# A hybrid decoder step: ScalarE's DMAs moved to GpSimd, the heads' query and key loads reordered and merged, and another pair of engines splitting the attention outputs

## The chip, the core and the metric

The kernel runs on one core of a Trainium2 chip. The metric is the device time of one execution in microseconds (us), from the median of several runs. The engines are TensorE (PE in the profile; PEld are its weight loads), VectorE (DVE), ScalarE (ACT), GpSimd (POOL) and SyncE (SP). Sixteen DMA engines serve the DMAs that SP, ACT and POOL issue.

## What is computed

One step of a one-layer decoder for 1024 prompt tokens and 64 sample tokens (8 sequences of 8) over a cache of 2048 keys: a half feed-forward block, then a mix of windowed softmax attention (12 heads of 64) and gated linear attention (GLA, 4 heads), then another half feed-forward block. All data is float32; matmuls run on float32r, each operand split into a high part and a remainder.

```python
def _half_ffn(x, gain, w1, w3, w2):
    h = _rmsnorm(x, gain)
    return x + 0.5 * ((jax.nn.silu(h @ w1) * (h @ w3)) @ w2)

z = h @ w_in                          # q, k, v, and the GLA inputs
logits = einsum(q, k) * Dh ** -0.5 + bias        # three dilated windows
p = jnp.exp(logits - lse[..., None])
o = einsum(p, v)                      # the windows' outputs merged by lse
```

## The kernel before

A tile framework allocates the buffers, puts a wait before each use of a buffer, and orders the instructions of every engine by a simulated timeline in which earlier code has priority. Inside one engine instructions run in the order so fixed. `_interleave` (L59) runs several generators beside each other, so that the work of one fills the gaps of another.

The time has four stages. Until about 821 us: the first feed-forward block and the norm. From 821 to 1244 us, the mix stage: `inputs` projects the tokens to q, k, v and gates (matmuls `psg`, L306), and `beside` does the sample attention at the same time. Here `turn_values` transposes the values on PE (`psv`), ACT copies them to SBUF (`v`, L431) and issues their stores `out_vp` (L439), `vnew` (L434) and `out_wv_s` (L435); `finish_gate` stores the gate `zr` to `gsc` from ACT (L446); `finish_qk` stores q and k to `qsc` and `out_kT` from POOL (L473). `beside` loads its bias tile `sbias` (L799) from SP with a source of shape 8 x 16 x 1288 whose first dimension has stride zero, so that 16 rows are copied 8 times; and it issues `sko` and `soT` stores from ACT.

From 1244 to 1519 us, the attention stage, `attention` (12 prompt heads) runs beside `linear_states` (GLA). For each head `load(h)` brings q from `qsc` and k from `out_kT` (L929), each twice, as two DMAs of 64 rows by 1024 floats into the lower and the upper half of one 128-row tile `f`. There is one `f` buffer for q and one for k. DVE rounds them (`q`, L932; `kk`, L934) and POOL subtracts the remainders (L933, L935; DVE does that for the first head). Then come the bias tile (L937) and, for every even head, the values `va` of a pair (L940). `load(h + 1)` is called while head h works on the second of its four groups. `linear_states` loads its tiles `g` (L596, L598) on the same SP queue, and DVE's first use of them is L611. DVE does the bias and the running minimum of the scores (L969), ACT the exponentials. When a pair has four groups of output `o`, `split` writes the high part into `hH` (L132, DVE) and the remainder into `hL` (L134, DVE).

From 1519 us `out_proj` (matmuls `pso`) reads `hH`, `hL` and its weights `hl`, which ACT casts and POOL subtracts (L130, L134) from `raw`; the second feed-forward block follows until 2400 us.

Waits for DMAs are on semaphores. The DMAs of SP and ACT take turns on one set of eight, those of POOL on another set of eight; a DMA is issued only when the one before it on its semaphore has landed.

Of the kernel before, what the change touches and what calls it, by code (L numbers as in the profile page):

```python
# [9 lines left out]
F32 = mybir.dt.float32  # L10
# [6 lines left out]
P = 128  # L17
NT = 1088
NP = 1024
# [66 lines left out]
class _Weights:  # L86
# [6 lines left out]
    def load(self, j, k=0, nk=8):  # L93
        if j < len(self.units):
            if k == 0:
                self.raw[j] = self.pool.tile(list(self.units[j].shape), F32, tag="raw", name="raw", bufs=self.deep)
            self.k.nc.sync.dma_start(out=self.raw[j][:, k : k + nk], in_=self.units[j][:, k : k + nk])
# [23 lines left out]
class _Kernel:  # L121
# [299 lines left out]
    def turn_values(self, pool, ps, z, m, ci):  # L421
        nc, a = self.nc, self.a
        cols = slice(128 * m, 128 * m + 128)
        t0, nt = 3 * ci, 3 if ci < 2 else 2
        p = ps.tile([P, 512], F32, tag="b", name="psv")
        for t in range(nt):
            nc.tensor.transpose(p[:, 128 * t : 128 * t + 128], z[:, 128 * t : 128 * t + 128], self.ident)
        if ci == 2:
            nc.tensor.transpose(p[:64, 256:384], z[:, 256:320], self.ident)
        v = pool.tile([P, 3, 128], F32, tag="t1", name="v", bufs=4)  # L430
        nc.scalar.copy(v[:, :nt].rearrange("p t c -> p (t c)"), p[:, : 128 * nt])  # L431
        if ci == 2:
            nc.scalar.copy(v[:64, 2], p[:64, 256:384])
            nc.scalar.dma_start(out=self.vnew[:, cols], in_=v[:64, 2])  # L434
            nc.scalar.dma_start(  # L435
                out=a["wv_s"].rearrange("b (r c) -> b r c", c=768)[:, 2040:2048, cols], in_=v[:64, 2]
            )
            self.vdone = m + 1
        nc.scalar.dma_start(  # L439
            out=a["vp"][128 * t0 : 128 * (t0 + nt), cols].rearrange("(t p) c -> p t c", p=P), in_=v[:, :nt]  # L440
        )

    def finish_gate(self, z, m, ci):
        nc = self.nc
        nc.scalar.activation(z, z, AF.Silu)
        nc.scalar.dma_start(  # L446
            out=self.gsc[3 * ci : 3 * ci + 3, :, 5 + m].rearrange("t p r -> p t r"),
            in_=z.rearrange("p (t r) -> p t r", t=3),
        )
# [131 lines left out]
    def linear_states(self, pool, ps):  # L581

        nc, a = self.nc, self.a
        st = pool.tile([P, 9, 64], F32, tag="st", name="st", bufs=2)
        nc.gpsimd.memset(st[:, 0], 0.0)
        ms = pool.tile([P, 3, 36], F32, tag="gms", name="gms")
        qm = []
        for z in range(2):
            t = pool.tile([P, 4, 8, 32], F32, tag="qm", name="qm", bufs=2)
# [46 lines left out]
        for T in range(9):  # L636
            g, kdT, bl = nxt
# [9 lines left out]
            p = ps.tile([P, 512], F32, tag="T", name="psR", bufs=4)  # L647
            for j, src in enumerate((kdT, g[:, 3], g[:, 4])):
# [3 lines left out]
                out=kx,  # L652
# [9 lines left out]
            p = ps.tile([P, 512], F32, tag="T", name="psD", bufs=4)  # L662
# [115 lines left out]
    def sample(self, pool, ps, loadk):  # L778
# [18 lines left out]
        for i in range(6):  # L797
# [8 lines left out]
            for e in range(2):  # L806
# [7 lines left out]
            nc.tensor.transpose(p[:64, :128], ks, self.ident)  # L814
            ko = pool.tile([64, 128], F32, tag="sko", name="sko", bufs=1)
            nc.scalar.copy(ko, p[:64, :128])
            nc.scalar.dma_start(
                out=a["wk"].rearrange("b (r c) -> b r c", c=768)[:, 2040:2048, 128 * i : 128 * i + 128], in_=ko
            )
            e = pool.tile([P, NKEY], F32, tag="se", name="se", bufs=1)  # L820
# [83 lines left out]
            t = pool.tile([64, 8, 2, 8], F32, tag="soT", name="soT", bufs=1)  # L904
            nc.scalar.copy(t, p[:64, :128].rearrange("p (b e t) -> p b e t", e=2, t=8))
            for e in range(2):
                nc.scalar.dma_start(
                    out=self.osc[i, 64 * e : 64 * e + 64].rearrange("p (b t) -> p b t", t=8), in_=t[:, :, e]
                )
            yield 100  # L910

    def attention(self, inputs, pool, ps):
        nc = self.nc
        heads = {}

        def load(h):
            i, e = h // 2, h % 2
            f = []  # L920
            for u, src in enumerate((self.qsc, self.a["kT"])):
                f.append(inputs.tile([P, NP], F32, tag="f", name="f", bufs=2))
                if u == 0:
                    q = inputs.tile([P, NP], F32R, tag="q", name="q", bufs=2)
                    b = inputs.tile([P, NP], F32, tag="bias", name="bias", bufs=2)
                    kk = inputs.tile([P, 2, NP], F32R, tag="kk", name="kk", bufs=2)
                    kh, kl = kk[:, 0], kk[:, 1]
                for w in range(2):
                    nc.sync.dma_start(out=f[u][64 * w : 64 * w + 64], in_=src[64 * h : 64 * h + 64])  # L929
            o = slice(64, 128)  # L930
            el = nc.gpsimd if h else nc.vector
            nc.vector.tensor_copy(q, f[0])  # L932
            el.tensor_tensor(out=q[o], in0=f[0][o], in1=q[o].bitcast(F32), op=ALU.subtract)  # L933
            nc.vector.tensor_copy(kh, f[1])  # L934
            el.tensor_tensor(out=kl, in0=f[1], in1=kh.bitcast(F32), op=ALU.subtract)  # L935
            z = self.Z[h]
            nc.sync.dma_start(out=b, in_=bass.AP(z.tensor, z.offset + 127, [[GW - 1, P], [1, NP]]))  # L937
            if e == 0:
                v = pool.tile([P, 8, 128], F32, tag="v", name="va", bufs=2)
                nc.sync.dma_start(  # L940
                    out=v, in_=self.a["vp"][:, 128 * i : 128 * i + 128].rearrange("(t p) c -> p t c", p=P)
                )
            else:
                v = heads[h - 1][3]
            heads[h] = (q, kh, kl, v, b)

        def scores(h, g):

            q, kh, kl, v, b = heads[h]
            out = []  # L950
            ss = pool.tile([P, 2, 4], F32, tag="s", name="s", bufs=6)
            for n in (2 * g, 2 * g + 1):
                w = 128 * (n + 1)
                e = pool.tile([P, w], F32, tag=f"e{n}", name="e", bufs=2 if n < 4 else 1)
                s = ss[:, n % 2]
                out.append((e, s, w))
                for j, o in enumerate(range(0, w, 512)):
                    m = min(512, w - o)
                    mm = max(m, 256)
                    p = ps.tile([P, 512], F32, tag="S", name="psS", bufs=2)  # L960
                    for x, kk in enumerate((kh, kl)):
                        self.mm(  # L962
                            p[:, :mm],
                            lhsT=q[:, 128 * n : 128 * n + 128],
                            rhs=kk[:, o : o + mm],
                            start=x == 0,
                            stop=x == 1,
                        )
                    nc.vector.tensor_tensor_reduce(  # L969
                        out=e[:, o : o + m],  # L970
                        in0=p[:, :m],
                        in1=b[:, 128 * (7 - n) + o : 128 * (7 - n) + o + m],
                        op0=ALU.add,
                        op1=ALU.min,
                        scale=-1.0,
                        scalar=BIG if j == 0 else s[:, 0:1],
                        accum_out=s[:, j : j + 1],
                    )
                    yield None
            for e, s, w in out:  # L980
                j = (w - 1) // 512
                nc.scalar.activation(  # L982
                    e[:, :w], e[:, :w], AF.Exp, scale=-1.0, bias=s[:, j : j + 1], accum_out=s[:, 2:3]
                )
            yield [e for e, s, w in out] + [ss]
# [23 lines left out]
        def weigh(h, g, es, pts):  # L1009
            i, e = h // 2, h % 2  # L1010
            r = slice(64 * e, 64 * e + 64)
            v = heads[h][3]
            if g % 2 == 0 and e == 0:
                outs[i, g // 2] = pool.tile([P, 512], F32, tag="o", name="o", bufs=3)
            p = ps.tile([P, 512], F32, tag="O", name="psO", bufs=2)
# [16 lines left out]
                nc.vector.tensor_tensor(out=outs[i, g // 2][r, c], in0=p[o, :128], in1=rb[o], op=ALU.mult)  # L1032
            if g % 2 and e == 1:
                z = slice(512 * (g // 2), 512 * (g // 2) + 512)
                self.split(outs.pop((i, g // 2)), self.hH[:, i, z], self.hL[:, i, z], eh="dve", el="dve")

        order = [(h, g) for h in range(12) for g in range(4)]
        lag = 3
        outs = {}
        self.tc.keep_in_program_order(nc.scalar.preload_act_table_set(LOG_EXP))  # L1040
        load(0)
        yield 10
        es = {}
        for x in range(len(order) + lag):
# [102 lines left out]
    def run(self):  # L1147
        nc, tc, a = self.nc, self.tc, self.a
        self.gready, self.done, self.vdone = False, 0, 0
        with ExitStack() as top:  # L1150
            self.dram = top.enter_context(tc.tile_pool(name="dram", bufs=1, space=DRAM))
            cp = top.enter_context(tc.tile_pool(name="const", bufs=1))
# [120 lines left out]
            with ExitStack() as hs:  # L1273
                hpool(hs)
                with ExitStack() as bs:
                    ip, gp = (bs.enter_context(pool(n)) for n in ("attin", "gst"))
                    ap = bs.enter_context(pool("att", side="right"))
                    ps0 = bs.enter_context(pool("ps", space=PSUM))
                    states = (4.6 * c for c in self.linear_states(gp, ps0))
                    _interleave(tc, [(self.attention(ip, ap, ps0), 0), (states, 0)])  # L1280
                with pool("wts") as wp, pool("xp", side="right") as xp:
                    w = _Weights(self, wp, [a["wout"][u] for u in range(4)] + w13b)
                    w.start()
# [163 lines left out]
```

## Time and profile before

| | before |
|---|---|
| median of 3 runs | 2398.7 us (2397.25 to 2399.25) |
| profiled execution | 2401.93 us |
| its span, first to last instruction | 2400.1 us |
| PE busy | 2341.4 us (98%) |
| DVE busy | 1155.9 us (48%) |
| ACT busy | 656.9 us (27%) |
| POOL busy | 408.3 us (17%) |
| mean granted PE clock | 0.989 |

A row of the timeline gives an instruction's start and length, its engine, line, operation, output and input, and in brackets the engine's idle time before it and what ended it. "ACTq" and "SPq" are the queues on which an engine issues DMAs. "PEclk" is the granted clock as a share of full speed. A share of the DMA engines can pass 1, since overlapping packets are each counted.

### The profile page before, as it was taken

How to read it: one execution, taken by the hardware profiler on the slowest of the kernel's cores; microseconds unless marked ns; L12 is line 12 of the kernel's file. 1: busy time of each engine (PE TensorE's matmuls, PEld its weight loads, DVE VectorE, ACT ScalarE, POOL GpSimd, SP SyncE). 2: the span in 40 equal slices, each digit the busy share in tenths (PEclk: the TensorE clock that was granted, in tenths of full speed). 3: DMA queues.
4: the chain of work that ended last, by engine and by line, in shares of the span. 5: the costliest groups of instructions: out<-in, count | busy, mean ns of one | idle time of the engine just before them, and what ended most of it. 6: DMA issues, size and time to landing. Idle time of an engine off the chain costs nothing.

```text
span 2400.1 us, 38321 instructions
## 1 busy us (share of the span) xinstructions
PE 2341.4 (98%) x16073; PEld 2215.0 (92%) x16073; DVE 1155.9 (48%) x2377; ACT 656.9 (27%) x1347; POOL 408.3 (17%) x303
## 2 busy tenths in 40 slices
PE   7999999999999998999989999999999999999999
PEld 6999999999999987978767767999999999999999
DVE  8452434344342753555538887435444342434333
ACT  5111020101101522545436666334111101020110
POOL 5011020101100400011103231333101101020100
PEclk9999999999999999999999999999999999999999
DMA  7346542524250334599865442414244243111002
GB/s 258 110 162 192 191 152 97 210 97 153 86 196 23 134 131 108 179 342 341 310 184 130 111 115 74 156 36 158 88 163 153 92 154 143 45 53 45 28 17 85
DMA packets 135261, 330.25 MB, mean 138 GB/s; under 512 B 25920, under 2 KB 105264, under 8 KB 127408
## 3 DMA queue, kind: packets, MB, share of 16 engines
q1 hardware_dynamic: 116464, 316.39, 38.7%
q10 hardware_dynamic: 16512, 5.11, 0.9%
q0 software_dynamic: 2112, 6.29, 0.7%
q8 instruction: 126, 2.06, 0.3%
q14 instruction: 47, 0.39, 0.0%
HBM read 300.55 MB, written 134.56 MB: 181 GB/s over the span
## 4 chain that ended last, share of the span: by engine, by line
PE 89%; DVE 5%; DMA 3%; ACT 2%; issue 1%; SPq 1%; POOL 0%; ACTq 0%; DVEq 0%; POOLq 0%
PE ps L306 42%; PE ps L257 21%; PE psg L306 12%; PE pso L306 4%; PE psO L1022 2%; PE psS L962 2%; PE psW L880 1%; PE psT L1001 1%; DMA vt<-in_vin 1%; PE psA L831 1%; DVE hL L155 1%; DVE e L969 1%; PE pss L459 1%; DMA f<-out_kT 0%; DVE rstd L170 0%
## 5 line engine op out<-in xcount | busy, mean ns | idle before, releaser
L306 PE MATMUL ps<-hH,hl 128*128 128x362 f32 (+1 forms) x4224 | 1044.1, 328 | 8.1 <-ACT hl L130 6.8
L306 PEld LDWEIGHTS ps<-hH,hl 128*128 128x128 f32 x4224 | 746.6, 188 | 12.4 <-ACT hl L130 6.7
L306 PE MATMUL ps<-hL,hl 128*128 128x362 f32 (+1 forms) x2112 | 691.5, 328 | 2.9 <-DVE hL L155 2.9
L257 PE MATMUL ps<-g,hl 128*128 128x362 f32 (+1 forms) x3168 | 529.2, 328 | 0.0
L257 PEld LDWEIGHTS ps<-g,hl 128*128 128x128 f32 x3168 | 527.0, 188 | 0.0
L134 POOL TENSOR_TENSOR hl<-raw,hl 128x1024 fp32r<-128x1024 f32 (+1 forms) x98 | 242.8, 2498 | 1223.3 <-ACT hl L130 1223.3
L306 PEld LDWEIGHTS ps<-hL,hl 128*128 128x128 f32 x2112 | 397.5, 188 | 4.9 <-DVE hL L155 3.9
L306 PE MATMUL psg<-hH,hl 128*128 128x384 f32 (+3 forms) x1200 | 312.4, 334 | 0.0
L262 DVE SCALAR_TENSOR_TENSOR xT<-ps,xT 128x362 f32<-128x362 f32 (+1 forms) x384 | 204.6, 534 | 200.3 <-PE ps L257 191.4
L217 ACT ACTIVATE t<-t 128x364 f32<-128x364 f32 x132 | 66.9, 508 | 786.0 <-DVE t L216 785.8
L218 DVE TENSOR_TENSOR t<-ps,rstd 128x364 f32<-128x364 f32 x132 | 70.6, 535 | 417.9 <-PE ps L306 417.9
L306 PEld LDWEIGHTS psg<-hH,hl 128*128 128x128 f32 (+1 forms) x1200 | 211.3, 186 | 12.8 <-issue 8.9
L306 PE MATMUL psg<-hL,hl 128*128 128x384 f32 (+3 forms) x600 | 200.1, 334 | 0.1
L130 ACT CAST hl<-raw 128x1024 fp32r<-128x1024 f32 (+2 forms) x148 | 124.1, 886 | 187.3 <-PE ps L306 109.9
L130 ACT CAST g<-t 128x364 fp32r<-128x364 f32 x132 | 65.2, 494 | 346.8 <-DVE t L219 346.8
L134 DVE TENSOR_TENSOR g<-t,g 128x364 fp32r<-128x364 f32 x132 | 107.1, 813 | 92.8 <-ACT g L130 92.5
L216 DVE TENSOR_TENSOR t<-ps,rstd 128x364 f32<-128x364 f32 x132 | 70.5, 535 | 156.6 <-PE ps L306 155.3
L306 PEld LDWEIGHTS psg<-hL,hl 128*128 128x128 f32 (+1 forms) x600 | 111.7, 186 | 9.3 <-issue 6.7
L134 DVE TENSOR_TENSOR hl<-raw,hl 128x384 fp32r<-128x384 f32 (+3 forms) x178 | 102.9, 587 | 23.9 <-ACT hl L130 19.9
L962 PE MATMUL psS<-kk,q 128*128 128x512 f32 (+2 forms) x288 | 92.2, 411 | 19.6 <-DVE s L969 11.9
L306 PE MATMUL pso<-hH,hl 128*128 128x362 f32 (+1 forms) x384 | 93.6, 325 | 0.2 <-DVE o L1032 0.2
L982 ACT ACTIVATE e<-e,s 128x128 f32<-128x128 f32 (+3 forms) x96 | 74.9, 780 | 43.7 <-DVE s L969 43.1
(205 smaller groups left out, 2007.2 us busy)
## 6 DMA issues: line engine op xcount, KB each, us to landing
out_wk<-in_ck SPq DMA_DIRECT2D x16, 3060.0 KB
out_wv_s<-in_cv SPq DMA_DIRECT2D x16, 3060.0 KB
kt<-in_kin SPq DMA_DIRECT2D x24, 1280.0 KB
vt<-in_vin SPq DMA_DIRECT2D x60, 512.0 KB
raw<-in_w13b SPq DMA_DIRECT2D x22, 1024.0 KB
raw<-in_w13a SPq DMA_DIRECT2D x21, 1024.0 KB
raw<-in_w2a SPq DMA_DIRECT2D x48, 192.0 KB
raw<-in_w2b SPq DMA_DIRECT2D x48, 192.0 KB
```

Source lines behind the costliest of these rows:

```text
L130: nc.scalar.copy(hi, x)
L134: e.tensor_tensor(out=lo, in0=x, in1=hi.bitcast(F32), op=ALU.subtract)
L155: nc.vector.scalar_tensor_tensor(out=self.hL[:, k, s], in0=x, scalar=g, in1=self.hH[:, k, s].bitcast(F32), op0=ALU.mult, op1=ALU.subtract)
L216: nc.vector.tensor_tensor(out=t1[:, :n], in0=p1[:, :n], in1=r, op=ALU.mult)
L217: nc.scalar.activation(t1[:, :n], t1[:, :n], AF.Silu)
L218: nc.vector.tensor_tensor(out=t3[:, :n], in0=p3[:, :n], in1=r, op=ALU.mult)
L257: self.mm(p[:, :n], lhsT=hl[:, wt, j, :], rhs=g[:, gp, :n], start=i == 0, stop=i == 3 * nf - 1)
L262: nc.vector.scalar_tensor_tensor(out=xs, in0=p[:, :n], scalar=0.5, in1=xs, op0=ALU.mult, op1=ALU.add)
L306: self.mm(p[:m, :n], lhsT=hl[:, wt, k, cs], rhs=h[:, k, h0 : h0 + n], start=i == 0, stop=i == 23)
L962: self.mm(p[:, :mm], lhsT=q[:, 128 * n : 128 * n + 128], rhs=kk[:, o : o + mm], start=x == 0, stop=x == 1,)
L982: nc.scalar.activation(e[:, :w], e[:, :w], AF.Exp, scale=-1.0, bias=s[:, j : j + 1], accum_out=s[:, 2:3])
L1022: self.mm(p[64 * n : 64 * n + 64, :128], lhsT=v[:, k, r], rhs=pts[k // 2][k, n], start=k == 0, stop=k == 2 * g + n, tile_position=(0, 64 * n),
```

## The change

- The stores that ACT issued in `turn_values`, `finish_gate`, and for `sko` and `soT` are issued by GpSimd: 18 `out_vp`, 6 `vnew`, 6 `out_wv_s`, 6 `zr`, 6 `sko` and 12 `soT`, 54 in all.
- The values' load stands in a function of its own. That of pair 0 is called at the start of `linear_states`, the others after the bias of their even head.
- Each head's q and k come in one DMA of 512 KB each instead of two of 256 KB. Its source has a first dimension of 2 with stride zero, so that the 64 rows are read twice.
- `load(0)` is given priority, and the GLA states come first in `_interleave`.
- The split of the attention outputs takes the defaults of `split`: the cast on ACT, the subtraction on GpSimd.

```diff
-            nc.scalar.dma_start(out=self.vnew[:, cols], in_=v[:64, 2])
-            nc.scalar.dma_start(
+            nc.gpsimd.dma_start(out=self.vnew[:, cols], in_=v[:64, 2])
+            nc.gpsimd.dma_start(
...
-        nc.scalar.dma_start(
+        nc.gpsimd.dma_start(
             out=a["vp"][128 * t0 : 128 * (t0 + nt), cols].rearrange("(t p) c -> p t c", p=P), in_=v[:, :nt]
...
         nc.scalar.activation(z, z, AF.Silu)
-        nc.scalar.dma_start(
+        nc.gpsimd.dma_start(
             out=self.gsc[3 * ci : 3 * ci + 3, :, 5 + m].rearrange("t p r -> p t r"),
...
         nc.gpsimd.memset(st[:, 0], 0.0)
+        self.load_v(pool, 0)
...
-                for w in range(2):
-                    nc.sync.dma_start(out=f[u][64 * w : 64 * w + 64], in_=src[64 * h : 64 * h + 64])
+                nc.sync.dma_start(
+                    out=f[u], in_=src[64 * h : 64 * h + 64].unsqueeze(0).broadcast_to([2, 64, NP])
+                )
...
-            if e == 0:
-                v = pool.tile([P, 8, 128], F32, tag="v", name="va", bufs=2)
-                nc.sync.dma_start(
...
+            if h % 2 == 0 and h:
+                load_v(i)
...
-                self.split(outs.pop((i, g // 2)), self.hH[:, i, z], self.hL[:, i, z], eh="dve", el="dve")
+                self.split(outs.pop((i, g // 2)), self.hH[:, i, z], self.hL[:, i, z])
...
-        load(0)
+        with self.tc.high_priority(offset=300):
+            load(0)
...
-                    _interleave(tc, [(self.attention(ip, ap, ps0), 0), (states, 0)])
+                    _interleave(tc, [(states, 0), (self.attention(ip, ap, gp, ps0), 0)])
```

How the order of the instructions changes is shown at three places. On SP at the start of the attention stage, before (`vt` are the cached values of the sample attention; L929 are the loads of `f`):

```order
L794 DMA vt<-in_vin 128x1024 x4
L940 DMA va<-out_vp 128x8x128 x2
L929 DMA f<-qsc 64x1024 x2
L929 DMA f<-out_kT 64x1024 x2
L937 DMA bias<-Z 128x1024
L596 DMA g_11144<-gsc 128x640
L598 DMA g_11144<-asc 128x4x128
```

and now:

```order
L795 DMA vt<-in_vin 128x1024 x4
L936 DMA f<-qsc 128x1x1024
L936 DMA f<-out_kT 128x1x1024
L946 DMA bias<-Z 128x1024
L917 DMA va<-out_vp 128x8x128
L597 DMA g_11129<-gsc 128x640
L599 DMA g_11129<-asc 128x4x128
```

The first head's loads stand ahead of the values, and two instructions take the place of four.

On ACT in the mix stage, at the second head pair's values, before:

```order
L431 COPY v<-psv 128x384
L543 ACTIVATE gd<-gd 128x648
L439 DMA out_vp<-v 128x3x128
L561 COPY band<-psL 128x18x11
L431 COPY v<-psv 128x256
L543 ACTIVATE gd<-gd 128x576
L433 COPY v<-psv 64x128
L439 DMA out_vp<-v 128x2x128
L434 DMA vnew<-v 64x128
L435 DMA out_wv_s<-v 8x8x128
```

and now:

```order
L431 COPY v<-psv 128x384
L543 ACTIVATE gd<-gd 128x648
L561 COPY band<-psL 128x18x11
L431 COPY v<-psv 128x256
L543 ACTIVATE gd<-gd 128x576
L433 COPY v<-psv 64x128
L543 ACTIVATE gd<-gd 128x504
L561 COPY band<-psL 128x18x10
```

No DMA stands between ACT's copies any more.

On ACT at the end of the attention stage (`hl<-raw` are the first weights of `out_proj`), before:

```order
L991 COPY dg<-s 128x128
L1004 COPY pt<-psT 128x512 x3
L1018 COPY rb<-psO 128x128
L130 CAST hl<-raw 128x1024 x4
L159 ACTIVATE rstd<-xT 128x364
```

and now:

```order
L998 COPY dg<-s 128x128
L1011 COPY pt<-psT 128x512 x3
L1025 COPY rb<-psO 128x128
L130 CAST hH<-o 128x512
L130 CAST hl<-raw 128x1024 x4
L159 ACTIVATE rstd<-xT 128x364
```

The last cast of an attention output stands ahead of the weights' casts. On POOL the last subtraction of an output stands ahead of the weights' subtractions in the same way.

## Rows read from the trace of the kernel before

**Rows 1.** Two stages: length, busy of PE, PEld, DVE, ACT, POOL; PEclk, DMA share, GB/s.

```profile
821.00:1244.00 423.00, 410.21 (x3041) 347.47 (x3039) 210.42 (x406) 168.63 (x352) 38.77 (x94) 0.98 0.69 232
1244.00:1519.00 275.00, 248.13 (x2903) 193.44 (x2903) 216.50 (x653) 181.36 (x479) 72.42 (x52) 0.94 0.41 112
```

**Rows 2.** Timeline of SP at the start of the attention stage.

```profile
1224.89 1.75 SPq L794 DMA_DIRECT2D vt<-in_vin  x4
1237.09 1.01 SPq L940 DMA_DIRECT2D va<-out_vp  x2
1238.26 6.00 SPq L929 DMA_DIRECT2D f<-qsc  x2
1245.28 1.11 SPq L929 DMA_DIRECT2D f<-out_kT  x2
```

**Rows 3.** Timeline of PE there, its first matmul of the stage.

```profile
1250.82 0.77 PE L962 MATMUL psS<-kk,q 128*128 128x256 f32 x2 [6.91 <-DVE kk L934]
```

**Rows 4.** DMA issues: count and KB of each.

```profile
f<-qsc SPq DMA_DIRECT2D x24, 256.0 KB
...
bias<-Z SPq DMA_DIRECT2D x12, 512.0 KB
...
va<-out_vp SPq DMA_DIRECT2D x6, 512.0 KB
...
g<-gsc SPq DMA_DIRECT2D x9, 320.0 KB
...
g<-asc SPq DMA_DIRECT2D x9, 256.0 KB
```

**Rows 5.** Timeline of SP, then three windows, around one sbias load (columns as rows 1).

```profile
929.23 11.89 SPq L575 DMA_DIRECT2D asc<-band  x4
941.22 3.91 SPq L799 DMA_DIRECT2D sbias<-sB  x1
...
942.00:945.00 3.00, 3.00 (x23) 3.00 (x23) 0.19 (x1) 0.00 (x0) 0.00 (x0) 1.00 0.52 18
946.60:948.80 2.20, 2.20 (x15) 2.20 (x14) 0.00 (x0) 0.00 (x0) 0.00 (x0) 1.00 0.54 131
954.00:957.00 3.00, 0.00 (x0) 0.00 (x0) 0.00 (x0) 0.00 (x0) 0.00 (x0) 0.50 1.03 412
```

**Rows 6.** Timelines of DVE and of SP inside the heads.

```profile
1327.12 0.29 DVE L611 TENSOR_TENSOR gw<-g 128x128 f32<-128x128 f32 x1 [2.10 <-DMA g<-gsc]
...
1336.73 0.69 DVE L932 CAST q<-f 128x1024 fp32r<-128x1024 f32 x1
...
1472.58 0.69 DVE L932 CAST q<-f 128x1024 fp32r<-128x1024 f32 x1
...
1340.27 1.10 SPq L929 DMA_DIRECT2D f<-qsc  x2
```

**Rows 7.** Timelines of ACT and PE in the mix stage, and POOL's line of stores there.

```profile
954.63 0.38 ACTq L439 DMA_DIRECT2D out_vp<-v  x1
...
957.51 0.48 ACT L431 COPY v<-psv 128x384 f32<-128x384 f32 x1 [20.20 <-DMA vt<-in_vin]
...
958.04 0.69 PE L427 MATMUL psv<-ident,zv 128*128 128x128 f32 x2 [8.77 <-ACT v L431]
...
L473 POOL DMA_DIRECT2D qsc<-z x18 | 10.0, 554 | 143.0 <-DVE z L468 143.0
```

**Rows 8.** DVE's two lines of the output split, 1244 to 1521 us: busy, mean ns.

```profile
L134 DVE TENSOR_TENSOR hL<-o,hH 128x512 fp32r<-128x512 f32 x12 | 15.1, 1259 | 0.1
...
L132 DVE CAST hH<-o 128x512 fp32r<-128x512 f32 x12 | 10.0, 832 | 0.1
```

**Rows 9.** Timelines of ACT, POOL and DVE at the end of the attention stage.

```profile
1516.21 3.92 ACT L130 CAST hl<-raw 128x1024 fp32r<-128x1024 f32 x4
...
1517.36 10.09 POOL L134 TENSOR_TENSOR hl<-raw,hl 128x1024 fp32r<-128x1024 f32 x4 [8.69 <-ACT hl L130]
...
1518.47 0.59 DVE L1032 TENSOR_TENSOR o<-psO,rb 64x128 f32<-64x128 f32 x2 [2.48 <-PE psO L1022]
```

More of the change, by code (lines that the diff above doesn't have):

```diff
@@ L816, in sample @@
             nc.scalar.copy(ko, p[:64, :128])
-            nc.scalar.dma_start(
+            nc.gpsimd.dma_start(
                 out=a["wk"].rearrange("b (r c) -> b r c", c=768)[:, 2040:2048, 128 * i : 128 * i + 128], in_=ko
@@ L906, in sample @@
             for e in range(2):
-                nc.scalar.dma_start(
+                nc.gpsimd.dma_start(
                     out=self.osc[i, 64 * e : 64 * e + 64].rearrange("p (b t) -> p b t", t=8), in_=t[:, :, e]
@@ L910, in sample, with load_v, attention @@
             yield 100
-    def attention(self, inputs, pool, ps):
+    def load_v(self, pool, i):
+        v = pool.tile([P, 8, 128], F32, tag="v", name="va", bufs=2)
+        self.nc.sync.dma_start(
+            out=v, in_=self.a["vp"][:, 128 * i : 128 * i + 128].rearrange("(t p) c -> p t c", p=P)
+        )
+        self.values[i] = v
+    def attention(self, inputs, pool, vpool, ps):
         nc = self.nc
@@ L927, in load @@
                     kh, kl = kk[:, 0], kk[:, 1]
-                for w in range(2):
-                    nc.sync.dma_start(out=f[u][64 * w : 64 * w + 64], in_=src[64 * h : 64 * h + 64])
+                nc.sync.dma_start(
+                    out=f[u], in_=src[64 * h : 64 * h + 64].unsqueeze(0).broadcast_to([2, 64, NP])
+                )
             o = slice(64, 128)
@@ L937, in load, with load_v @@
             nc.sync.dma_start(out=b, in_=bass.AP(z.tensor, z.offset + 127, [[GW - 1, P], [1, NP]]))
-            if e == 0:
-                v = pool.tile([P, 8, 128], F32, tag="v", name="va", bufs=2)
-                nc.sync.dma_start(
[L941 to L945, printed above, removed]
+            if h % 2 == 0 and h:
+                load_v(i)
+            heads[h] = (q, kh, kl, b)
+        def load_v(i):
+            self.load_v(vpool, i)
         def scores(h, g):
-            q, kh, kl, v, b = heads[h]
+            q, kh, kl, b = heads[h]
             out = []
@@ L1011, in weigh @@
             r = slice(64 * e, 64 * e + 64)
-            v = heads[h][3]
+            v = self.values[i]
             if g % 2 == 0 and e == 0:
@@ L1149, in run @@
         self.gready, self.done, self.vdone = False, 0, 0
+        self.values = {}
         with ExitStack() as top:
```

## The prediction

> **What bounds the kernel now.** The first view to read is the table of stages [rows 1]. TensorE is busy 410 of 423 us in the mix stage and 248 of 275 us in the attention stage; in the other two stages, which the change leaves alone, it hardly stops. So there are only two places where a change can win: 13 us of idle time in the mix stage and 27 us in the attention stage. Nobody else is near his limit there: VectorE has 216 of 275 us, and the DMA engines work at 0.41 of their capacity. The second thing to read is the largest single stop in either stage. In the mix stage it is 8.77 us, for ACT's copy of the values [rows 7]; at the start of the attention stage it is 6.91 us, for the first head's keys [rows 3]. The third is the DMA view, for what each load of the attention stage carries [rows 4], and the windows round a load of the sample bias [rows 5], which is the one load of the old kernel written like the new head loads.
>
> **The stores moved from ACT to GpSimd: -9 us.** ACT copied its values late, at 957.51, after 20.20 us without work; the row puts that down to a DMA of cached values, yet in ACT's own queue a store `out_vp` stands issued at 954.63, and the copy follows it [rows 7]. The store's turn came only when an earlier DMA of the shared set, a load of SP's, had landed. GpSimd's DMAs have a set of their own and ACT has no DMA left there, so the 8.77 us for which TensorE waited go. What is late next? The operands of those transposes were ready, so nothing I can see; I take 9 us, as the clock stands at 0.50 in that stop [rows 5] and recovers after it. The ends are 0, should the store's place be taken by a wait for a buffer, and 11. The other side: 54 stores go to GpSimd. Its own stores cost 554 ns each [rows 7]; at that price they add 30 us, and at four times that, for stores of smaller pieces, 120 us. It is busy 39 of 423 us [rows 1], so both fit.
>
> **The merged head loads: +67 us.** This is the term that decides. 48 DMAs of 256 KB [rows 4] (the keys' row reads the same) become 24 of 512 KB, whose source begins with a dimension of two copies. The bias load `sbias` begins with eight copies in the same manner. It was issued at 941.22 and held until 945.13; while it ran alone, the DMA engines were busy at 0.54, that is 8.6 of 16, and moved 131 GB/s, where plain loads reach 1.03 and 412 GB/s [rows 5]. I read that as: the copies, not the rows, are dealt out to the engines, one engine for each copy. Against it speaks the store `asc`, whose first dimension is 4 and which also shows 0.52 [rows 5]; but it moves 18 GB/s in tiny pieces, and the share counts overlapping packets more than once (1.03), so it counts no engines. Two copies then mean two engines. At 412/16 = 25.75 GB/s each, 524,288 bytes take 524,288 / 51,500 = 10.2 us. At the rate of the bias load, 131/8 = 16.4 GB/s for each engine, it is 16.0 us; if the reading is wrong, the load takes 1.3 us at 412 GB/s. I take 10.2, since the pieces of 4 KB are those of the plain loads, and only two engines read the same rows at a time, where eight did.
>
> [...]
>
> Now the sum over the stage. 24 x 10.2 = 245 us of head loads run through the two engines one after another, since one queue feeds them. The plain loads put a sixteenth on each engine too: 12 of 512 KB, 6 of 512 KB, 9 of 320 and 9 of 256 KB [rows 4], 14.7 MB in all, 36 us at 412 GB/s. That is 281 us for a stage of 275. The first head load can be issued once the last cached values are, at 1226.64 [rows 2]; these are four of 512 KB, 5 us, so it starts at 1231. If the engines never paused, the last keys would land at 1231 + 281 = 1512. They do pause. The query buffer is single: the next load waits for DVE's cast and GpSimd's subtraction, 3.5 us from 1336.73 to 1340.27 [rows 6]. Mostly the other load fills that gap. Where DVE must first use a gate tile, which is queued behind both head loads, it doesn't: 9.6 us pass between that use and the next cast (1327.12 to 1336.73 [rows 6]), and 3.5 + 1.1 more until the load is out, 14 us. Three of the nine gate tiles stand so in the middle of a head; of their 42 us I take 28, as bias and values still run in some. The last keys land at 1540. Today the last query cast is at 1472.58 and the stage ends at 1519, 46.4 us later [rows 6]; DVE takes its instructions in order, so the cast of the last head cannot move ahead. The stage ends near 1586 by the clock of the old profile, 67 us late; without the pauses 39 us late, and at 16.0 us a load (384 + 36 us of loads) 206 us late. I take 67.
>
> What covered the loads before? From 1336.73 to 1472.58 lie six heads, 22.6 us each [rows 6], so that a load issued at 1340.27 had some 19 us until its cast. That cover holds one load of 10.2 us, and not two behind each other.
>
> **The first head first: in the term above.** Today the first queries' second half is issued only at 1244.26, after 6.00 us of waiting for a semaphore that ACT's store held, behind the values [rows 2]. The change takes that wait away and would win about 6.5 of the 6.91 us [rows 3] with fast loads. With slow ones the keys land at 1231 + 20.4 = 1251.4, no earlier than today.
>
> **The split of the outputs: +4 us.** DVE loses 25.1 us [rows 8], work that no longer stands between its score passes. In a stage bound by loads that is worth nothing; by itself up to 5 us. On ACT a cast of 512 columns costs half of 3.92/4, so 0.5 us, on GpSimd half of 10.09/4, so 1.3 us [rows 9]. At the end they lie in front of work that TensorE needs: the last output is ready at 1519.06 [rows 9]; ACT's cast then ends at 1519.6 and the first weights' at 1520.6, GpSimd's two subtractions at 1520.9 and 1523.4. Before, the weights were ready ahead of the output; now `out_proj` begins about 4 us later. The ends are 1 (later heads' slack lets the weights go first) and 10 (four subtractions in a row).
>
> **Sum.** 2401.9 - 9 + 67 + 4 = 2463.9 us for the profiled execution (its own 2401.93 us, a span of 2400.1 and 1.8 us around it), which stands 3.2 us over the median of 2398.7; 2461 us as a median.
>
> **Rivals.** First, *the loads are not confined* (1.3 us each). Then the kernel is faster: 2401.9 - 9 - 6.5 - 5 + 4 - 3.2 = 2382 us. For it speaks that the same bytes move and the queue has fewer instructions; against it the 0.54 and 131 GB/s of the like-made load. Chance 0.08. Second, *the two head loads use different pairs of engines*. No row names an engine. Then both land 10.2 us after issue, inside the cover of 19 us; what is left is the gate tiles behind them, three times 8 us, and the first head gains 6.5: 2401.9 - 9 - 6.5 + 24 + 4 - 3.2 = 2411 us. Chance 0.08. Third, *each engine is as slow as in the bias load*, 16.0 us: 2401.9 - 9 + 206 + 4 - 3.2 = 2600 us. Chance 0.10; rates between lie between. Fourth, *GpSimd becomes the bound*: its stores delay its own `out_kT` and remainders, and it decides once a store costs over 423 - 39 = 384 us / 54 = 7 us, nowhere near 554 ns. Chance 0.02, about 2420 us. Short stops in the attention stage also drop the clock to 0.50, as here [rows 5]; TensorE has slack while loads bind, so 0 to 10 us on top.
>
> **How the numbers follow.** The forecast, loads confined to one pair of engines at nearly full rate, has 0.72. Its own range is 2430 (no pauses: 39 in place of 67, and 1 for the tail) to 2520 (a load at 12 us, 43 us more over 24 loads; clock and tail at their upper ends). The range of 8 in 10 goes down to the second rival: 2411 to 2520. Left out are the faster case below and the slow rate above. About 0.2%, some 5 us, is what can be told from no change: faster 0.08, within 0.01, slower 0.91.
>
> **What would show it.** In the profile after, the head loads' group shows 24 of 512 KB, and in windows inside the attention stage the DMA share lies near 2/16 for long stretches, at some 50 GB/s; that is the step that carries all. DVE's casts `q` and `kk` wait for `f`, and the time between casts of neighbouring heads is near 27 us, where it was 22.6. The attention stage is some 65 to 75 us longer. In the mix stage the 8.77 us are gone and ACT has no store between its copies. `out_proj` begins 3 to 5 us after the last output, waiting for weights. If the casts find their loads landed, and the share during a load is near 1, the first rival is right and the kernel is faster.

## The result, and the profile after

The changed kernel takes 2481.55 us (2480.49 to 2483.59, 4 runs), the kernel before 2398.97 us: a ratio of 1.0342 (95% interval 1.0327 to 1.0358), 82.6 us slower. The forecast was 2461 us in a range of 2411 to 2520. The page of the changed kernel begins:

```profile
span 2478.7 us, 38332 instructions
PE 2357.7 (95%) x16073; PEld 2227.4 (90%) x16073; DVE 1131.0 (46%) x2353; ACT 662.7 (27%) x1359; POOL 456.8 (18%) x369
...
PEclk9999999999999999999968899999999999999999
...
PE 84%; DMA 10%; DVE 3%; ACT 1%; POOL 1%; issue 1%; SPq 0%; DVEq 0%; ACTq 0%; POOLq 0%
```

The third line is the granted clock by slices, the last the chain that ended last: DMAs held 3% of it before and hold 10% now. By stages (columns as in [rows 1]) the trace of the changed kernel reads:

```profile
821.00:1234.00 413.00, 408.65 (x3040) 344.90 (x3039) 210.64 (x406) 169.07 (x353) 74.16 (x147) 1.00 0.69 236
1234.00:1595.20 361.20, 262.92 (x2904) 204.90 (x2902) 198.23 (x631) 185.10 (x489) 84.38 (x65) 0.84 0.27 87
```

The last matmul of the mix stage starts at 1234.0, where it was 1243.6, so this stage gives back some 10 us. The first matmul of the output projection starts at 1595.2; before, at 1518.3. The attention stage, with its start, grew from 274.7 to 361.2 us, by 86.5. From there to the end both kernels take nearly the same time (881.8 and 883.5 us). The account is -9.6 + 86.5 + 1.7 = 78.6 us, the difference of the spans. The medians differ by 4 us more, because the execution traced before (2401.93 us) lay 3 us above its median and the one traced after 1 us below.

Where the 86.5 us are is shown by the list of DVE's waits in that stage (total, times, longest):

```profile
DVE kk L943 <- DMA f<-out_kT: 47.9, 9, 9.6
DVE gw L612 <- DMA g<-gsc: 37.7, 5, 16.3
DVE e L976 <- PE psS L969: 27.4, 41, 2.9
DVE q L941 <- DMA f<-qsc: 13.8, 3, 6.7
```

The casts of the keys and queries wait 61.7 us for their loads, and the first use of a gate tile waits 37.7 us; before, the latter was 7.1. The same list of the kernel before has:

```profile
DVE gw L611 <- DMA g<-gsc: 7.1, 5, 3.4
...
DVE q L932 <- DMA f<-qsc: 2.8, 1, 2.8
...
DVE kk L934 <- DMA f<-out_kT: 0.8, 2, 0.4
```

TensorE no longer sets the pace. What the DMA engines do while a head load runs alone, and in two pauses, stands in these windows (columns as in [rows 1]):

```profile
1266.00:1276.00 10.00, 2.50 (x6) 1.45 (x6) 1.67 (x7) 2.90 (x7) 2.17 (x1) 0.50 0.13 53
...
1345.50:1351.00 5.50, 5.50 (x54) 4.12 (x54) 4.88 (x14) 4.45 (x12) 1.75 (x3) 0.64 0.00 0
1379.00:1390.00 11.00, 8.59 (x53) 6.44 (x55) 7.96 (x27) 8.80 (x20) 0.63 (x2) 0.79 0.00 0
```

A share of 0.13 is two of sixteen, and 53 GB/s is 26.5 for each, so that 524,288 bytes take 9.9 us. The plain load of the kernel before had 1.03 and 412 GB/s [rows 5].

### The profile page after: what moved, and what is told of

It is laid out like the page before. It is cut to its first block, busy times and chain, and to the rows that moved or that the text cites. A ratio compares the mean times of both kernels' runs of the same rounds, so it can differ in the third digit from the quotient of the medians.

```text
span 2478.7 us, 38332 instructions
## 1 busy us (share of the span) xinstructions
PE 2357.7 (95%) x16073; PEld 2227.4 (90%) x16073; DVE 1131.0 (46%) x2353; ACT 662.7 (27%) x1359; POOL 456.8 (18%) x369
## 4 chain that ended last, share of the span: by engine, by line
PE 84%; DMA 10%; DVE 3%; ACT 1%; POOL 1%; issue 1%; SPq 0%; DVEq 0%; ACTq 0%; POOLq 0%
PE ps L306 41%; PE ps L257 20%; PE psg L306 12%; DMA f<-out_kT 8%; PE pso L306 4%; PE psA L832 1%; DMA g<-gsc 1%; PE psW L881 1%; DMA va<-out_vp 1%; DVE hL L155 1%; PE psO L1029 1%; PE psS L969 1%; POOL kk L944 1%; DMA vt<-in_vin 1%; PE psT L1008 1%
## 5 line engine op out<-in xcount | busy, mean ns | idle before, releaser
L969 PE MATMUL psS<-kk,q 128*128 128x512 f32 (+2 forms) x288 | 99.8, 440 | 52.0 <-DVE s L976 38.2
L969 PEld LDWEIGHTS psS<-kk,q 128*128 128x128 f32 x288 | 50.7, 218 | 65.3 <-DVE s L976 33.9
```

Source lines behind the costliest of these rows:

```text
L969: self.mm(p[:, :mm], lhsT=q[:, 128 * n : 128 * n + 128], rhs=kk[:, o : o + mm], start=x == 0, stop=x == 1,)
```

## The experiments

Each was compared with the kernel before on its own chip; the ratio carries its 95% interval. "Changed kernel" is the one of the result above.

**1. Two loads again.** In the changed kernel:

```diff
-                nc.sync.dma_start(
-                    out=f[u], in_=src[64 * h : 64 * h + 64].unsqueeze(0).broadcast_to([2, 64, NP])
-                )
+                for w in range(2):
+                    nc.sync.dma_start(out=f[u][64 * w : 64 * w + 64], in_=src[64 * h : 64 * h + 64])
```

> The changed kernel, with each head's q and k again in two loads of 64 rows (no source dimension of two copies); all other parts of the change stay. Theory (the merged loads run on two of sixteen engines and set the pace): the load term goes and the gains remain, so the mix stage is 9 to 10 us shorter than in the kernel before, the first keys land at once, and the time is 2380 to 2390 us. Rival (another part of the change, its order of loads or the stores on GpSimd, makes the loss): the time stays over 2450 us.

Measured: 2385.01 us, ratio 0.9934 (0.9921 to 0.9946). With this one edit undone the change is a gain of 16 us, near the 2382 us of the first rival, whose loads run on all engines. The merge alone costs some 97 us inside the changed kernel. TensorE's wait for the first keys is 3.2 us there. The mix stage is 7.3 us shorter in this trace, less than the 9 to 10 that were expected.

**2. The merged loads alone.** The edit of experiment 1 the other way round, in the kernel before.

> The kernel before, with the merged q and k loads alone. Theory: the loss is there without any other part, 2465 to 2490 us, with DMA share 0.13 and about 53 GB/s while one head load runs alone. Rival (the merge costs only together with the new order): under 2420 us.

Measured: 2509.77 us, ratio 1.0454 (1.0438 to 1.047); some 109 us slower, more than was expected. The mechanism stands (the first row is a window with one head load alone), and the excess is where the next rows show it: gate tiles are waited for longer than in the changed kernel, and TensorE waits 22.5 us for the first keys, where it is 13.2 in the changed kernel. Their load stands behind the values in SP's queue there and is issued only at 1242.19, 5 us after the queries' load; the changed kernel issued it at 1218.36.

```profile
1268.00:1278.00 10.00, 5.44 (x30) 4.09 (x29) 4.35 (x15) 5.27 (x19) 0.46 (x1) 0.84 0.13 52
```

```profile
DVE gw L611 <- DMA g<-gsc: 56.4, 6, 17.7
DVE kk L935 <- DMA f<-out_kT: 54.1, 9, 10.1
...
PE psS L963 <- DVE kk L935: 22.5, 1, 22.5
```

**3. The stores alone.** In the kernel before, the six places at which ACT issues a DMA:

```diff
-        nc.scalar.dma_start(
+        nc.gpsimd.dma_start(
```

> The kernel before, with ACT's 54 stores issued by GpSimd and nothing else. Theory: TensorE's stop of 8.8 us in the mix stage goes, and at the start of the attention stage the 6 us for which SP waited on the semaphore of ACT's store: 2383 to 2390 us. Rival (the copy was late because of the cached values, as its row says): within 3 us of 2399.

Measured: 2390.89 us, ratio 0.9962 (0.9949 to 0.9974), about 10 us faster; the end of what was expected is just missed. The late copy is gone. In this run's timeline of ACT the copies of values follow each other by about 4.5 us:

```profile
948.49 0.37 ACT L431 COPY v<-psv 128x256 f32<-128x256 f32 x1 [3.35 <-issue]
...
953.00 0.48 ACT L431 COPY v<-psv 128x384 f32<-128x384 f32 x1 [3.98 <-issue]
...
957.53 0.47 ACT L431 COPY v<-psv 128x384 f32<-128x384 f32 x1
```

Before, nothing was copied between 937.3 and 957.5, and the store was issued only at 954.63 [rows 7]. That row names a DMA of cached values as releaser. The run shows that it was the store: the cached values are loaded as before, and the stop is gone. In the trace of the kernel before, ACT's stores there wait on the semaphores of SP's loads: `out_vp` on that of the `sbias` load until 954.6, `out_wv_s` on that of a load of cached values until 956.80, which the row names. Issuing the first pair of head loads took 6.00 us [rows 2] and takes 2.32 here; a free pair takes 1.1, so the wait for the semaphore shrank from 4.9 to 1.2 us. TensorE still waits 5.7 us for the first keys; the values' load, issued at 1227.00, stands ahead of them. On GpSimd the new stores take 0.56 to 0.76 us each, as means by line.

```profile
936.25 0.71 POOL L439 DMA_DIRECT2D out_vp<-v  x1 [2.93 <-ACT v L433]
936.96 0.56 POOL L434 DMA_DIRECT2D vnew<-v  x1
937.51 0.62 POOL L435 DMA_DIRECT2D out_wv_s<-v  x1
```

**4. The split back on DVE**, in the kernel of experiment 1:

```diff
-                self.split(outs.pop((i, g // 2)), self.hH[:, i, z], self.hL[:, i, z])
+                self.split(outs.pop((i, g // 2)), self.hH[:, i, z], self.hL[:, i, z], eh="dve", el="dve")
```

> The kernel of the first run of this call, with the output split back on DVE. Theory: the split on ACT and GpSimd costs 2 to 4 us at the end of the attention stage and gives back less than 3 us inside it, so this run lies 0 to 3 us under the first. Rival (DVE was the bound of the attention stage once the loads are fast): this run lies 5 us or more above the first.

Measured: 2387.56 us, ratio 0.9949 (0.9937 to 0.9962), 2.6 us above experiment 1. The sign is against the theory: with fast loads the split on ACT and GpSimd gives a little more than it costs. DVE isn't the bound either. The five times of each run don't overlap (2384.0 to 2385.7 us in experiment 1, 2387.2 to 2391.0 here), so the sign is clear. The size is not: between the two traces, 2.2 us already stand at the end of the mix stage, which this edit leaves alone.

**5 and 6. Another number of copies.** As many bytes into the same tile, read as 4 copies of 32 rows, and as 16 copies of 8 rows. The other rows of each head are left out, so these two kernels compute other scores and serve for their times alone:

```diff
-                    out=f[u], in_=src[64 * h : 64 * h + 64].unsqueeze(0).broadcast_to([2, 64, NP])
+                    out=f[u], in_=src[64 * h : 64 * h + 32].unsqueeze(0).broadcast_to([4, 32, NP])
...
+                    out=f[u], in_=src[64 * h : 64 * h + 8].unsqueeze(0).broadcast_to([16, 8, NP])
```

> The changed kernel, its head loads with a source of 4 copies of 32 rows in place of 2 copies of 64 (same bytes, same tile; rows 32 to 63 of q and k are left out, so the scores are of other data). Theory (one engine for each copy): a load takes 5.1 us on four engines, DMA share 0.25 and about 105 GB/s while it runs alone, so that the loads fit under a head again: 2385 to 2400 us. Rival (any merged load with a repeated source is slow, whatever the number of copies): over 2450 us.

> As the run before, with 16 copies of 8 rows (rows 8 to 63 of q and k are left out). Theory: all sixteen engines, share near 1, a load is as fast as two of 64 rows: 2380 to 2388 us, as with the two loads. Rival (repeated source): over 2450 us; half way, if reading the same row at the same time is slow by itself: 2400 to 2440 us.

Measured: 2420.27 us (1.0087, 1.0071 to 1.0104) with 4 copies and 2383.05 us (0.9929, 0.9914 to 0.9944) with 16. So neither the merge nor the repeated source is slow; what counts is how many copies there are. A window of the run with 4 and one of the run with 16, each while one load runs alone:

```profile
1247.00:1252.00 5.00, 4.88 (x94) 3.57 (x95) 3.00 (x12) 2.78 (x8) 0.00 (x0) 1.00 0.25 99
...
1256.00:1258.00 2.00, 1.83 (x14) 1.27 (x15) 1.91 (x8) 1.99 (x6) 1.77 (x1) 1.00 1.01 250
```

The first is four of sixteen and 24.8 GB/s for each. In the second all engines are busy, and the load, issued at 1254.74, moves nearly all its bytes in these 2 us. The time with 4 copies was expected up to 2400 and is 20 us above that: the loads hardly hold up their own casts any more (15.1 us), but the gate tiles behind them still do:

```profile
DVE gw L612 <- DMA g<-gsc: 26.6, 5, 10.0
...
DVE kk L943 <- DMA f<-out_kT: 9.2, 3, 4.8
...
DVE q L941 <- DMA f<-qsc: 5.9, 2, 3.3
```

**7. Only the queries merged**, the keys in two loads, in the changed kernel.

> The changed kernel, with only the q load merged and k again in two loads of 64 rows. Theory (a load had some 19 us of cover, which holds one load of 10.2 us and not two in a row): 12 x 10.2 + 36 to 60 us of loads is well under the stage's 260, so little is lost: 2388 to 2405 us, some for gate tiles queued behind the slow load. Rival (each slow load costs its full length): half the loss, about 2433 us.

Measured: 2442.18 us, ratio 1.0174 (1.0159 to 1.0189). This theory fell: one slow load per head costs 57 us, more than half of what two cost and 9 us above the rival's 2433.

```profile
DVE gw L612 <- DMA g<-gsc: 40.9, 6, 10.9
...
DVE q L944 <- DMA f<-qsc: 23.3, 4, 10.8
```

**8. The gate tiles' loads on GpSimd**, in the changed kernel (L597 and L599 on `nc.gpsimd`), so that they pass the head loads in SP's queue.

> The changed kernel, with the loads of the gate tiles (L597, L599) issued by GpSimd, so that they don't stand behind the head loads in SP's queue. Theory (DVE's waits for gate tiles queued behind head loads stop the next loads, 20 us or more in all): these waits shrink and the time falls by 12 to 30 us, to 2452 to 2470 us. Rival (the loads' own length sets everything, the waits are only its sign): within 6 us of 2481.

Measured: 2476.04 us (2469.36 to 2478.29), ratio 1.0312 (1.0294 to 1.0329). The waits for gate tiles fell from 37.7 to 8.5 us; those for keys rose from 47.9 to 61.5. Of nearly 30 us taken away some 6 are left in the time: less than the theory expected, and within the rival's 6 us of 2481. What one stop released the next one took: the loads' own length is close behind.

```profile
DVE kk L943 <- DMA f<-out_kT: 61.5, 11, 12.3
...
DVE gw L612 <- DMA g<-gsc: 8.5, 3, 3.5
```

**9. Both: only the queries merged, and the gate tiles on GpSimd.**

> Only the q load merged, as in the run that gave 2442 us, and the gate tiles' loads issued by GpSimd, so that they don't queue behind it. Theory (a covered load of 10.2 us costs nothing by itself; what it costs is that it holds up the gate tiles behind it, for which DVE then stood 40.9 us): 2390 to 2405 us. Rival (the slow load's own length costs, whoever waits): within 8 us of 2442.

Measured: 2425.08 us, ratio 1.0097 (1.0081 to 1.0113), between the two: 17 us of the 57 come back, 40 stay. The times of DVE's query casts say where. Between the casts of heads 0 and 2 the two-load kernel of experiment 1 takes 20.9 us (1237.2, 1247.9, 1258.1), this one 41.1 (1237.55, 1261.08, 1278.61): at the start two heads are loaded ahead at 10 us each, and there is no cover of 19 us. That is 20 of the 40. Head 5 takes 7 more than in the two-load kernel (30.9 against 23.8): ACT waits for the sample outputs `so`, a plain load that stands behind a query load in SP's queue.

```profile
1261.08 0.69 DVE L944 CAST q<-f 128x1024 fp32r<-128x1024 f32 x1 [3.74 <-DMA f<-qsc]
...
1278.61 0.69 DVE L944 CAST q<-f 128x1024 fp32r<-128x1024 f32 x1 [9.07 <-DMA f<-qsc]
```

```profile
1343.95 0.51 ACT L130 CAST hH<-so 128x384 fp32r<-128x384 f32 x1 [12.37 <-DMA so<-osc]
```

The rest, some 13 us over nine heads, isn't settled; GpSimd, which now issues these loads in its own order, waits 14.6 us for their buffers, and may have its part.

**10. The very last split on DVE**, in the kernel of experiment 1:

```diff
-                self.split(outs.pop((i, g // 2)), self.hH[:, i, z], self.hL[:, i, z])
+                e = dict(eh="dve", el="dve") if (i, g) == (5, 3) else {}
+                self.split(outs.pop((i, g // 2)), self.hH[:, i, z], self.hL[:, i, z], **e)
```

> The changed kernel with two loads of 64 rows, and the very last split of an attention output on DVE, the other eleven on ACT and GpSimd. Theory (that one cast stands in front of the first weights of the output projection and costs 2.4 us): 2382 to 2384 us, 1 to 3 us under the 2385 us of the two-load kernel. Rival (the stop moves to the remainder on GpSimd or to DVE): no difference.

Measured: 2380.56 us, ratio 0.9919 (0.9905 to 0.9933), the fastest kernel here, 19.7 us under the kernel before and a little below what was expected. The stop at the first weights is gone; first the list of TensorE's waits in experiment 1, then in this run:

```profile
PE pso L306 <- ACT hl L130: 2.4, 1, 2.4
```

```profile
PE pso L306 <- DVE o L1038: 0.2, 1, 0.2
```

The two ratios overlap, so the times alone don't prove the 2 us; the waits show that the stop is gone.

**11. The merged loads issued by GpSimd**, in the changed kernel (`nc.gpsimd` at L936).

> The changed kernel with its merged head loads issued by GpSimd in place of SP. Theory (the loss comes from all head loads running on the same two engines one after another): if loads of this queue go to changing pairs of engines, two run side by side and the time falls to 2400 to 2440 us. Rival (the same two engines here too): 2475 us or more, GpSimd's own waits on top.

Measured: 2450.37 us, ratio 1.0198 (1.0177 to 1.0219), 31 us less than from SP and outside both expectations. The DMA view gives the time from issue to landing for this queue:

```profile
f<-qsc POOLq DMA_DIRECT2D x12, 512.0 KB, 14.6
f<-out_kT POOLq DMA_DIRECT2D x12, 512.0 KB, 15.0
```

The two are issued within 1 us of each other in ten heads of twelve, and both land after about 15 us. A window in which only the two loads of one head are under way shows them at once:

```profile
1286.00:1288.00 2.00, 2.00 (x23) 1.48 (x22) 0.88 (x3) 1.59 (x4) 0.00 (x0) 0.87 0.27 106
```

That is four of sixteen and twice the 53 GB/s of one load. So from here they do run side by side, and the loss is smaller. Two waits in GpSimd's own order keep it from being less: it issues the first loads only at 1241.95, behind its stores, so that TensorE waits 24.7 us for the first keys, and it waits 15.6 us with the second query load, for DVE.

## Why the prediction was right, and where its sizes were off

**The step that carries all held.** The head loads, whose source begins with two copies, kept two of sixteen engines busy: a share of 0.13, 53 GB/s and 9.9 us, where 10.2 were forecast. The share is near 2/16 for long stretches, as was said: in 189 of the 312 us from 1234 to 1546 it lies between 0.10 and 0.16 (windows of 1 us). The query casts follow each other by 27.6 us on average, where 27 was said. The step was read from one row, the bias load with eight copies [rows 5], and experiments 5 and 6 turn that reading into a measured line: 2 copies 53 GB/s, 4 copies 99, and with 16 a share of 1.01 and the time of plain loads. The row itself was thin ground: its window is 2.2 us long, and in the half microseconds from 946.5 to 948.5 its share runs from 0.29 to 0.68. That the mean came out at eight engines was partly luck. Its 16.4 GB/s for each engine, the ground of the third rival, did not carry over: the head loads have 26.5. The objection, the store `asc` with 0.52 at 18 GB/s, was put aside, and the loads bear that out; why that store shows 0.52 is open. One DMA in place of two costs nothing with 16 copies (2383 against 2385 us) and some 97 us with 2 (experiment 1).

**The loop was longer than its sum.** Forecast were 67 us for the head loads and 4 for the split; together with the start, the attention stage grew by 86.5. Three casts of the changed kernel's DVE timeline, of the first queries, the first keys and the last keys:

```profile
1235.54 0.69 DVE L941 CAST q<-f 128x1024 fp32r<-128x1024 f32 x1 [0.59 <-DMA f<-qsc]
...
1246.80 0.69 DVE L943 CAST kk<-f 128x1024 fp32r<-128x1024 f32 x1 [9.31 <-DMA f<-out_kT]
...
1546.38 0.69 DVE L943 CAST kk<-f 128x1024 fp32r<-128x1024 f32 x1 [5.70 <-DMA f<-out_kT]
```

The first head explains a part: its queries were issued at 1217.62 and cast at 1235.54, its keys at 1246.80, where the forecast, shifted by the mix stage's gain, had them at 1241.8. The last keys were cast at 1546.38; shifted in the same way, the forecast was 1530. From the last keys to the output projection it is 48.8 us, against 46.4 and 4 for the split. So the 16 us that are missing lie between the first load and the last. My sum had 23.4 us of traffic per head (281 / 12) and 28 us of pauses. The chain of waits of the changed kernel (start, length, what) has in its second half one step that repeats, from GpSimd's remainder of one head's keys to that of the next:

```profile
1395.71 20.85 DMA f<-out_kT
1417.41 2.35 POOL kk L944
1419.78 23.49 DMA f<-out_kT
1444.12 2.34 POOL kk L944
1446.49 19.95 DMA f<-out_kT
...
1523.84 22.52 DMA f<-out_kT
```

From 1395.71 to 1523.84 that is 25.6 us for each of five heads: a key load that must first let its query load through (20 to 23 us), and the cast and subtraction that free the single key buffer. The term that was mis-sized is thus the pace: 25.6 in place of 23.4 us, 26 over twelve heads. The pauses with no traffic at all, in the windows above, are 17 us where I took 28. 12 x 25.6 + 17 = 324 us, and from the forecast start (1221.4 when shifted) to 1546.4 it is 325. The pace was read from late heads; the first six key casts lie 21.8 to 40.5 us apart, so there it holds only as a mean. Two errors cancelled in part: 26 us too few for the pace, 11 too many for the pauses. How the 5 us per head beyond the two loads divide into plain loads and waiting isn't separated.

**The cover.** That some 19 us hide one load of 10.2 us was wrong as a general statement, and was the ground of the second rival's 2411 us. Experiments 7 and 9 show why: the 19 us come from a mean over six late heads, while the casts of the first heads lie only some 10 us apart (experiment 9), and plain loads queued behind the slow one come late too: DVE waited 40.9 us for gate tiles in experiment 7, and ACT 12.37 us for `so` in experiment 9. From GpSimd, where the loads do run side by side, it is 2450 us. The forecast itself used the cover only to say that two loads don't fit.

**The stores moved from ACT** were forecast at -9 us. The mix stage is 9.6 us shorter, and alone they give about 10. In the traces of the ten other runs with these stores on GpSimd the stage is 4.2 to 10.4 us shorter than before, and TensorE waits there 0.2 to 3.8 us for cached values, so that the size was met to the half microsecond is luck. The reading that a store in ACT's queue, not the named DMA, held the copy, is confirmed by experiment 3. GpSimd, busy for 74 of 413 us, was no bound.

**The first head first** was counted in the loads' term: no gain with merged loads, about 6.5 us if they ran on all engines. With the merged loads TensorE waits even longer, 13.2 us in place of 6.91 [rows 3]; with two loads per tile the stop is 3.2 us (experiment 1), 3.7 us gained and not 6.5. The 6.00 us read as waiting contain the 1.1 us that a free pair of DMAs takes to issue.

**The split** was forecast at +4 us, of which the end of the stage shows 2.4. In the changed kernel the last cast of an output stands on ACT before the weights' cast, as was said:

```profile
1593.62 0.62 ACT L130 CAST hH<-o 128x512 fp32r<-128x512 f32 x1 [2.75 <-DVE o L1039]
1594.14 3.88 ACT L130 CAST hl<-raw 128x1024 fp32r<-128x1024 f32 x4
...
1595.23 0.67 PE L306 MATMUL pso<-hH,hl 128*128 128x364 f32 x1 [2.35 <-ACT hl L130]
```

TensorE waited for ACT alone. That it would also wait for GpSimd's remainder of the weights was the part that failed: no wait for it stands in the list of TensorE's waits. With fast loads the split gives back some 2 to 3 us more than that by the times of experiment 4.

**The clock** was to add 0 to 10 us. It is 0.84 in the attention stage, where it was 0.94; as loads bind there, no run separates its cost.

## What to carry to other kernels

Fewer and larger DMAs were not faster by themselves here (2481.55 us with merged head loads, 2385.01 with two each): look at the outermost dimension of the source. One that began with 2 or 4 copies left most of the engines idle, with a DMA share of 0.13 and 0.25 while a load ran alone, that is copies / 16; with 16 copies it was 1.01. The slow loads also delayed the loads behind them in SP's queue: DVE waited 37.7 us for gate tiles, where it had waited 7.1, and 8.5 with the gate tiles' loads on GpSimd (experiment 8). So price a load by the whole queue and the tightest gap between uses, not by the mean gap. Where a row names a DMA as releaser of an engine that issues DMAs itself, see whether its own issue was waiting.

## What the runs showed of the hardware

Two DMAs of the same form, one issued from SP and one from GpSimd, used the engines differently. From SP the queries and keys of a head came one after the other (the first head's casts at 1235.54 and 1246.80, 11.3 us apart, though issued 0.74 us apart); from GpSimd both landed about 15 us after an issue at nearly the same time, and for two of these microseconds the share was 0.27 and the rate 106 GB/s (experiment 11). So two loads from GpSimd kept four of sixteen engines busy at once, where the loads from SP kept two (0.13, 53 GB/s). Which engines a load took isn't shown, since no row names one. The forecast added up the lengths of all head loads because one queue feeds them. SP's queue bears that out, GpSimd's doesn't. That a load took 14.6 us from issue to landing in GpSimd's queue, where 9.9 us of transfer would do, is only partly explained: for loads issued at 1281.92 and 1282.74, the stretch from 1283 to 1284 still shows 3 GB/s.
